# Copying the sum of an output norm out of PSUM before the inverse square root

## The chip, the cores and the metric

One core of one Trainium2 chip runs the kernel. The metric is device time in microseconds of one execution: 2615.6 us, the median of three runs (2614.31 to 2616.1). Engines are called as in the profile: PE is the matrix engine (PEld its weight load), DVE the vector engine, ACT the scalar engine, POOL the general-purpose engine, SP the one that issues most transfers.

## The reference

The block works on 1024 tokens of width 1024 in float32: a half-step SwiGLU, a mixer, a half-step SwiGLU, a final RMS norm. The mixer adds two gated branches. One is gated linear attention (GLA) with 4 heads of value width 256, the other a gated delta rule with 8 heads of width 128, both in chunks. The output of every head goes through an RMS norm before it is gated:

```
oh = o.reshape(b, t, heads, -1)
oh = oh * rsqrt(mean(oh * oh, axis=-1) + EPS) * w
```

Here is the place of the change: the mean over the channels of a head, and the inverse square root of it.

## The kernel before, in words

Activations are kept transposed, channels on the 128 partitions and tokens along the free dimension, so a sum over the channels of a head is a sum over partitions. `out_rms` (L801) forms it with a product by a matrix of ones: `sq` (128x512, the squares, which a DVE instruction at L1058 or L1184 has put together) goes in, and a PSUM bank `q` holds the sum on every partition. The scalar engine then takes the logarithm of `q` (L805), the exponential of minus half of it (L806) and the square of that (L807). The logarithm and the exponential each have a table load of their own ahead of them. Two DVE instructions make one Newton step: L808 reads `q` again, with the square, and L809 ends the factor `y`. The caller multiplies the head's output by it (L1060 or L1187).

`out_rms` is called 24 times. `delta_rec` (L1018) calls it twice for each of the 8 delta heads, once for each half of the tokens (some 870 to 1355 us of the trace). `gla_rec` (L1132) calls it twice for each of the 4 GLA heads (some 1424 to 1790 us).

**Banks of PSUM.** In the delta stage the pool has 4 banks of tag `q` and 2 tiles of two banks of tag `ps`. The `q` banks serve everything small: the steps of the recurrence (L1034, L1038, L1047), the output `qo` of half a head (held until L1060), the sum in `out_rms`, and, for the next head, the transposed keys (L897, read by ACT at L901 and by DVE at L903) and the scores of `delta_prep` (L923, read by DVE at L925 and L929). In the GLA stage there are 2 `q` banks, 4 banks of tag `m` for the large products (L368) and one `ps` tile. There, too, the scores (L1152), the transposed keys (L1146, read by ACT at L1147) and the steps of the state (L1170) share the `q` banks with `out_rms`. The helper `half()` gives SBUF tiles `h` of 128x512, 4 of them; `sq`, `t` and `y` are of that kind.

**What sets the order.** Each engine runs its instructions in a fixed order, which a planner lays down when the program is built: it goes by the order of the text, by its own estimate of every instruction's time, by priorities (`tc.high_priority`) and by when a buffer comes free. In some places the text pins an instruction behind another one (`pinned`, `tc.issue_after`): the scores at L923 go behind a set step of a dense projection (L139). So the dense products are laid between the small products of the recurrence, and a buffer that comes free at another time can change the order of everything behind it.

Of the kernel before, what the change touches and what calls it, by code (L numbers as in the profile page):

```python
# [10 lines left out]
AF = mybir.ActivationFunctionType  # L11
ALU = mybir.AluOpType
# [727 lines left out]
def mixer(st, sto, tc, pool, start, xs, load_unit, dense, ptile, bank, rsqrt_newton, split, new_x, accumulate,  # L740
          ounits, dram, pr, ident, ones, cst, eye, wlr, win, wout, y_d, h_d, sqrt_table, strassen_products, rp, psum, divide, recent, pinned, run):
    nc = tc.nc
# [36 lines left out]
    def half():  # L779
        return sp.tile([P, 512], F32, name="h", tag="h", bufs=4)  # L780
# [20 lines left out]
    def out_rms(sq):  # L801
        q = bank()
        nc.tensor.matmul(out=q, lhsT=ones, rhs=sq, start=True, stop=True)
        t, y = half(), half()
        nc.scalar.activation(out=t, in_=q, func=AF.Ln)  # L805
        nc.scalar.activation(out=y, in_=t, func=AF.Exp, scale=-0.5)  # L806
        nc.scalar.activation(out=t, in_=y, func=AF.Square)  # L807
        nc.vector.scalar_tensor_tensor(out=t, in0=q, scalar=-0.5, in1=t, op0=ALU.mult, op1=ALU.mult)  # L808
        nc.vector.scalar_tensor_tensor(out=y, in0=t, scalar=1.5, in1=y, op0=ALU.add, op1=ALU.mult)  # L809
        return y  # L810

# [208 lines left out]
    def delta_rec(kq, qsq, vt3, gl, kst, qk, cj, yi):  # L1020
# [4 lines left out]
        for b in range(2):  # L1025
            qo = bank()
            for n in range(4):
# [17 lines left out]
                if c < NCH - 1:  # L1045
# [5 lines left out]
                    else:  # L1051
# [5 lines left out]
            nc.scalar.activation(out=osq, in_=qo, func=AF.Square, scale=P ** -0.5)  # L1057
            nc.vector.scalar_tensor_tensor(out=osq, in0=osq, scalar=EPS * EPS, in1=qsq[:, cc], op0=ALU.add, op1=ALU.add)  # L1058
            fac = out_rms(osq)
            nc.vector.scalar_tensor_tensor(out=oT[:, cc], in0=qo, scalar=ph[:, 98:99], in1=fac,  # L1060
                                           op0=ALU.mult, op1=ALU.mult)
# [70 lines left out]
    def gla_rec(la, kt, f, vtok):  # L1132
# [5 lines left out]
        for b in range(2):  # L1138
# [41 lines left out]
            for a in range(2):  # L1180
                sq = half()
                nc.scalar.activation(out=sq, in_=qo[a], func=AF.Square, scale=1.0 / 16)
                sqs.append(sq)
            nc.vector.scalar_tensor_tensor(out=sqs[0], in0=sqs[0], scalar=EPS / P, in1=sqs[1], op0=ALU.add, op1=ALU.add)  # L1184
            fac = out_rms(sqs[0])
            for a in range(2):
                nc.vector.scalar_tensor_tensor(out=o[a][:, cc], in0=qo[a], scalar=ph[:, 96 + a:97 + a],  # L1187
# [57 lines left out]
    for b in range(2):  # L1245
        q = bank()
# [94 lines left out]
    for g in range(4):  # L1341
# [11 lines left out]
        for a in range(2):  # L1353
            t = 2 * g + a
# [120 lines left out]
```

## Time and profile before

| | |
|---|---|
| median of 3 runs | 2615.6 us (2614.31 to 2616.1) |
| the profiled execution | 2616.17 us, its span 2614.4 us |
| PE busy | 2491.3 us, 95% of the span |
| DVE busy | 1872.5 us, 72% |
| POOL busy | 1168.2 us, 45% |
| ACT busy | 1065.2 us, 41% |
| granted TensorE clock, mean | 0.986 |
| bytes moved | 75 GB/s over the span |

Read the shares as averages over stages. With PE at 95% what counts is where PE stands still and what ends each standstill; idle time of the other engines costs nothing unless PE waits for them. The tables of waits give, for an engine and a line, how long it stood before that line and what released it.

### The profile page before, as it was taken

The numbers are of one execution on the slowest core, as the hardware profiler recorded it, in microseconds if no ns is written. First come the engines' busy times: TensorE is split into PE (matmuls) and PEld (weight loads), VectorE is DVE, ScalarE is ACT, GpSimd is POOL, SyncE is SP. The second block draws the span as 40 slices with busy tenths as digits, with TensorE's granted clock in tenths as the row PEclk, the third lists the DMA queues.
The fourth block names the chain that finished last, engine by engine and source line by source line (L and its number), as shares of the span: only waits on it lengthen the run. The fifth ranks groups of instructions, "written<-read, shape, count | busy, mean of one in ns | idle before, by whom it ended". The sixth has DMA issues, their size and how long they took to land.

```text
span 2614.4 us, 32722 instructions
## 1 busy us (share of the span) xinstructions
PE 2491.3 (95%) x11668; PEld 2021.0 (77%) x11668; DVE 1872.5 (72%) x2900; ACT 1065.2 (41%) x1841; POOL 1168.2 (45%) x1308
## 2 busy tenths in 40 slices
PE   7899999899999999999989999999989999998998
PEld 6788888677877877777767777878868888886677
DVE  8855555899676778887596666757586555569996
ACT  5333334333353444444345544535233333343331
POOL 4544444555217567676452122122144444446531
PEclk8999999999999999999999999999989999999999
DMA  3222222322322222212211212124212222213222
GB/s 118 73 73 85 92 71 72 125 81 77 117 73 73 65 61 65 61 45 53 65 51 37 80 39 85 57 65 138 73 35 78 88 74 85 89 61 115 79 89 81
DMA packets 93603, 199.05 MB, mean 76 GB/s; under 512 B 12248, under 2 KB 17112, under 8 KB 93440
## 3 DMA queue, kind: packets, MB, share of 16 engines
q1 hardware_dynamic: 82576, 175.64, 20.7%
q0 software_dynamic: 8704, 18.89, 2.8%
q10 hardware_dynamic: 2160, 2.43, 0.3%
q8 instruction: 92, 1.51, 0.2%
q14 instruction: 71, 0.58, 0.1%
HBM read 158.73 MB, written 38.17 MB: 75 GB/s over the span
## 4 chain that ended last, share of the span: by engine, by line
PE 72%; DVE 14%; ACT 5%; issue 3%; POOL 1%; DMA 1%; DVEq 0%; POOLq 0%; ACTq 0%
PE q L368 28%; PE ps L139 17%; PE m L368 10%; PE q L575 7%; PE q L1001 2%; DVE wl L127 2%; PE q L923 1%; DVE h L580 1%; DVE xl L127 1%; DVE ha L580 1%; DMA s<-a_d 1%; ACT L806 1%; PE q L1014 1%; DVE acc L794 1%; PE ps L1163 1%
## 5 line engine op out<-in xcount | busy, mean ns | idle before, releaser
L127 DVE TENSOR_TENSOR wl<-raw,wh 128x512 fp32r<-128x512 f32 (+1 forms) x243 | 209.0, 860 | 169.7 <-ACT wh L126 168.0
L139 PE MATMUL ps<-xl,wh 128*128 128x512 f32 (+2 forms) x768 | 266.6, 407 | 18.6 <-ACT wh L120 8.2
L139 PE MATMUL ps<-xh,wl 128*128 128x512 f32 (+2 forms) x768 | 266.8, 406 | 0.1
L139 PE MATMUL ps<-xh,wh 128*128 128x512 f32 (+1 forms) x768 | 263.6, 405 | 0.0
L127 DVE TENSOR_TENSOR wl<-sr,wh 128x512 fp32r<-128x512 f32 x226 | 200.1, 886 | 73.4 <-ACT wh L126 72.9
L368 PE MATMUL q<-xl,wh 128*128 128x512 f32 x640 | 249.0, 389 | 0.3 <-ACT c L374 0.3
L368 PE MATMUL q<-xh,wh 128*128 128x512 f32 x640 | 249.0, 389 | 0.0
L368 PE MATMUL q<-xh,wl 128*128 128x512 f32 x640 | 249.0, 389 | 0.0
L126 ACT CAST wh<-sr 128x512 fp32r<-128x512 f32 x226 | 140.0, 620 | 242.2 <-PE q L575 63.5
L473 POOL TENSOR_TENSOR s<-s,ysc 128x512 f32<-128x512 f32 x80 | 112.4, 1416 | 244.1 <-ACT s L472 244.1
L126 ACT CAST wh<-raw 128x512 fp32r<-128x512 f32 (+1 forms) x243 | 144.1, 593 | 173.8 <-PE q L368 95.4
L139 PEld LDWEIGHTS ps<-xl,wh 128*128 128x128 f32 (+1 forms) x768 | 144.9, 193 | 51.2 <-DVE xl L239 8.9
L356 POOL TENSOR_TENSOR raw<-sr 128x512 f32<-128x512 f32 x19 | 25.6, 1347 | 318.1 <-DMA sr<-in_win 226.1
L139 PEld LDWEIGHTS ps<-xh,wl 128*128 128x128 f32 (+1 forms) x768 | 145.8, 193 | 25.6 <-issue 1.0
L139 PEld LDWEIGHTS ps<-xh,wh 128*128 128x128 f32 x768 | 144.4, 192 | 25.5 <-issue 1.2
L368 PEld LDWEIGHTS q<-xl,wh 128*128 128x128 f32 x640 | 120.1, 188 | 25.5 <-issue 0.7
L368 PEld LDWEIGHTS q<-xh,wl 128*128 128x128 f32 x640 | 120.1, 188 | 24.9
L368 PEld LDWEIGHTS q<-xh,wh 128*128 128x128 f32 x640 | 120.1, 188 | 24.9
L379 DVE TENSOR_TENSOR c<-c,q 128x512 f32<-128x512 f32 x120 | 82.4, 686 | 74.0 <-PE q L368 74.0
L374 ACT COPY c<-q 128x512 f32<-128x512 f32 x120 | 70.4, 587 | 152.6 <-PE q L368 150.7
L948 POOL TENSOR_TENSOR xp<-xp,itmp 128x112 f32<-128x112 f32 (+29 forms) x248 | 122.5, 494 | 19.4
L945 POOL TENSOR_TENSOR itmp<-lt,xp 128x112 f32<-128x112 f32 (+29 forms) x248 | 110.1, 444 | 38.7 <-DMA lt<-l_d 19.9
(494 smaller groups left out, 6775.6 us busy)
## 6 DMA issues: line engine op xcount, KB each, us to landing
sr<-in_win SPq DMA_DIRECT2D x76, 256.0 KB, 2.6
a_d<-s SPq DMA_DIRECT2D x36, 512.0 KB, 3.7
raw<-in_win SPq DMA_DIRECT2D x70, 256.0 KB, 2.6
raw<-in_d SPq DMA_DIRECT2D x56, 256.0 KB, 2.7
raw<-in_g SPq DMA_DIRECT2D x48, 256.0 KB, 2.6
s<-a_d SPq DMA_DIRECT2D x24, 512.0 KB, 4.1
sr<-in_u SPq DMA_DIRECT2D x44, 256.0 KB, 2.9
raw<-in_u SPq DMA_DIRECT2D x44, 256.0 KB, 2.6
```

What stands on the lines that cost most here:

```text
L126: a = nc.scalar.copy(out=hi, in_=src)
L127: b = (eng or nc.vector).tensor_sub(out=lo, in0=src, in1=hi.bitcast(F32))
L139: mm = nc.tensor.matmul(out=ps[:m, sl], lhsT=w[:, :m], rhs=x[:, sl], start=(i == 0 and a == 0), stop=(i == n - 1 and a == 2))
L368: nc.tensor.matmul(out=ps, lhsT=p[:, c], rhs=q, start=(first and k == 0 and a == 0), stop=(k == 3 and a == 2), skip_group_check=not first)
L374: marks[0] = nc.scalar.copy(out=t, in_=ps).ins
L379: marks[1] = nc.vector.tensor_add(out=t, in0=t, in1=ps).ins
L473: nc.gpsimd.tensor_mul(out=s, in0=s, in1=y)
L575: nc.tensor.matmul(out=ps, lhsT=p[:, c], rhs=q, start=(first and k == 0 and a == 0), stop=(k == 1 and a == 2), skip_group_check=not first)
L580: nc.vector.scalar_tensor_tensor(out=hd[:, sl], in0=ps, scalar=0.5, in1=hd[:, sl], op0=ALU.mult, op1=ALU.add)
L945: inv_eng.tensor_tensor(out=tv, in0=lp[:, j, j + 1:].unsqueeze(2).broadcast_to([P, r, m]), in1=xp[:, j, :m].unsqueeze(1).broadcast_to([P, ...
L948: inv_eng.tensor_tensor(out=xv, in0=xv, in1=tv, op=ALU.subtract)
L1001: nc.tensor.matmul(out=q[:, c], lhsT=lhs[:, c], rhs=rhs[:, c], start=True, stop=True)
```

## The change

Inside `out_rms` the sum is copied from the bank `q` into `sq`, whose content the product has then consumed, with one DVE instruction. The logarithm and the first Newton instruction read the copy in place of the bank. Nothing else differs.

```diff
     def out_rms(sq):
         q = bank()
         nc.tensor.matmul(out=q, lhsT=ones, rhs=sq, start=True, stop=True)
+        nc.vector.tensor_copy(out=sq, in_=q)
         t, y = half(), half()
-        nc.scalar.activation(out=t, in_=q, func=AF.Ln)
+        nc.scalar.activation(out=t, in_=sq, func=AF.Ln)
         nc.scalar.activation(out=y, in_=t, func=AF.Exp, scale=-0.5)
         nc.scalar.activation(out=t, in_=y, func=AF.Square)
-        nc.vector.scalar_tensor_tensor(out=t, in0=q, scalar=-0.5, in1=t, op0=ALU.mult, op1=ALU.mult)
+        nc.vector.scalar_tensor_tensor(out=t, in0=sq, scalar=-0.5, in1=t, op0=ALU.mult, op1=ALU.mult)
         nc.vector.scalar_tensor_tensor(out=y, in0=t, scalar=1.5, in1=y, op0=ALU.add, op1=ALU.mult)
         return y
```

## Rows read from the trace of the kernel before

**Rows 1.** The page's first part: busy time and share of the span by engine.
```profile
PE 2491.3 (95%) x11668; PEld 2021.0 (77%) x11668; DVE 1872.5 (72%) x2900; ACT 1065.2 (41%) x1841; POOL 1168.2 (45%) x1308
```

**Rows 2.** Busy time by window: stretch, its length, PE, PEld, DVE, ACT, POOL.
```profile
860.00:1370.00 510.00, 484.69 (x2626) 388.07 (x2624) 395.39 (x783) 224.56 (x406) 321.52 (x589) 0.99 0.21 59
1370.00:1810.00 440.00, 424.25 (x2002) 344.81 (x2001) 299.63 (x459) 216.32 (x348) 105.14 (x75) 0.99 0.21 67
```

**Rows 3.** PE's waits, 860 to 1370 us: releaser, total us, times, longest.
```profile
PE q L923 <- DVE h L808: 6.7, 6, 1.3
...
PE q L1038 <- DVE rw L1036: 3.7, 5, 1.0
```

**Rows 4.** PE's waits, 1370 to 1810 us.
```profile
PE q L1152 <- DVE h L808: 4.0, 3, 1.3
```

**Rows 5.** The chain that ended last, 860 to 1370 us, by line.
```profile
by line: PE ps L139 41.7%; PE q L1001 10.9%; PE q L923 4.4%; PE q L1038 2.9%; PE q L1014 2.8%; PE q L1042 2.6%; ACT L805 2.3%; ACT L806 2.3%; PE q L1034 2.1%; PE q L1047 2.1%; PE q L1044 2.0%; issue 1.7%; PE q L983 1.4%; DVE h L808 1.4%; DV
```

**Rows 6.** The timeline, second half of one delta head: start, length, engine, line.
```profile
955.69 1.02 PE L803 MATMUL q<-h,cs 128*128 128x512 f32 x2
...
956.82 2.02 DVE L988 TENSOR_TENSOR kq<-kq,gb 128x1792 f32<-128x1792 f32 x1
...
958.10 0.60 ACT L805 ACTIVATE h<-q 128x512 f32<-128x512 f32 x1
...
961.05 0.62 ACT L807 ACTIVATE h<-h 128x512 f32<-128x512 f32 x1
...
961.70 0.69 DVE L808 SCALAR_TENSOR_TENSOR h<-q,h 128x512 f32<-128x512 f32 x1 [2.86 <-ACT h L807]
...
962.36 0.69 DVE L903 TENSOR_TENSOR kst<-q,kdec 128x512 f32<-128x512 f32 x1
962.45 1.59 PEld L923 LDWEIGHTS q<-kq 128*128 128x128 f32 x8 [1.38 <-DVE h L808]
962.45 1.99 PE L923 MATMUL q<-kq 128*128 128x256 f32 x8 [0.96 <-DVE h L808]
```

**Rows 7.** The timeline, first half of a GLA head.
```profile
1644.10 1.12 PE L803 MATMUL q<-h,cs 128*128 128x512 f32 x2
...
1645.79 0.60 ACT L805 ACTIVATE h<-q 128x512 f32<-128x512 f32 x1
...
1648.22 1.57 DVE L127 TENSOR_TENSOR wl<-sr,wh 128x512 fp32r<-128x512 f32 x1 [2.42 <-ACT wh L126]
...
1650.83 0.69 DVE L808 SCALAR_TENSOR_TENSOR h<-q,h 128x512 f32<-128x512 f32 x1 [1.04 <-ACT h L807]
...
1651.57 1.16 PE L1152 MATMUL q<-la,lt 128*128 128x128 f32 x8 [1.34 <-DVE h L808]
```

**Rows 8.** The timeline, first half of a delta head.
```profile
1001.28 1.13 PE L803 MATMUL q<-h,cs 128*128 128x512 f32 x2
...
1002.04 0.74 DVE L794 SCALAR_TENSOR_TENSOR acc<-ps,ph,acc 128x511 f32<-128x511 f32 x1
...
1002.70 0.28 DVE L1036 TENSOR_TENSOR rw<-vt,q 128x128 f32<-128x128 f32 x1
...
1003.03 0.33 PEld L1038 LDWEIGHTS q<-rw,yi 128*128 128x128 f32 x2
```

**Rows 9.** Groups of DVE by line and shape: count, busy us, mean ns, idle before.
```profile
L809 DVE SCALAR_TENSOR_TENSOR h<-h 128x512 f32<-128x512 f32 x24 | 19.5, 812 | 0.4
...
L808 DVE SCALAR_TENSOR_TENSOR h<-q,h 128x512 f32<-128x512 f32 x24 | 16.5, 687 | 24.6 <-ACT h L807 24.6
...
L1173 DVE COPY Sg<-q 128x256 f32<-128x256 f32 x4 | 1.7, 424 | 0.1
...
L1217 DVE COPY yi<-ps 72x512 f32<-72x512 f32 x1 | 0.7, 680 | 0.0
```

**Rows 10.** Groups of ACT by line and shape.
```profile
L806 ACT ACTIVATE h<-h 128x512 f32<-128x512 f32 x24 | 15.2, 632 | 0.3
...
L805 ACT ACTIVATE h<-q 128x512 f32<-128x512 f32 x24 | 14.4, 598 | 1.5 <-PE q L803 1.3
```

## The prediction

> **What bounds the kernel now.** Read the busy shares first: PE is busy for 95% of the span and DVE for 72% [rows 1]. PE sets the time, so the change can give back only what PE now stands idle. The table by stretch says how much that is where `out_rms` runs: in the delta stage PE is busy 484.69 of 510 us, 25.3 us idle; in the GLA stage 424.25 of 440, 15.8 us idle [rows 2]. Next read PE's waits in these stretches. The largest single one of the delta stage is the scores at L923 waiting for DVE's L808: 6 times, 6.7 us [rows 3]; in the GLA stage the scores at L1152 wait for the same line, 3 times, 4.0 us [rows 4]. L808 makes nothing that the scores read. It is the last reader of the bank `q` of `out_rms`, so this is a wait for a free bank. The chain that ended last agrees: in the delta stage it goes through the two steps of the inverse root on ACT, L805 and L806 with 2.3% each, and L808 with 1.4% [rows 5].
>
> The timeline of one head shows why the bank is held. The sum is done at 955.69 + 1.02 = 956.71; the logarithm starts at 958.10, the square at 961.05, L808 at 961.70, and the scores at 962.45, PE having stood for 0.96 us [rows 6]. So the bank is kept for 962.39 - 956.71 = 5.7 us after the sum is there. In the GLA stage it is the same: sum done at 1645.22, L808 ends at 1651.52, PE idle for 1.34 us [rows 7].
>
> **The change part by part.** Durations are from the profiled execution of 2616.17 us (span 2614.4 us); it lies 0.6 us above the median of 2615.6, so I take 0.6 off the sum at the end.
>
> *The wait for the bank.* With the copy the bank comes free when the copy ends, some 0.7 us after the sum, in place of 5.7 us. That is before PE reaches the scores in all nine places. What can be won is bounded by 0 (another wait takes its place in full) and by the whole 6.7 + 4.0 = 10.7 us [rows 3, 4].
>
> For the GLA stage I take all 4.0: the scores' inputs are long there, and the product behind them (L1170) needs a key tile that ACT makes, not L808. For the delta stage I take 4.5 of 6.7, for this reason: L923 x8 is two groups of four, each with its own bank. The second group starts near 962.45 + 1.0 = 963.45, and its bank comes from L903, which ends at 962.36 + 0.69 = 963.05 [rows 6]. It has 0.4 us to spare. If PE comes 0.96 us earlier, it waits 0.96 - 0.4 = 0.56 us for L903 in the same place. If the planner keeps the two groups together, 6 x 0.56 = 3.4 us of the 6.7 come back, and 3.3 are won; if it parts them with dense products, as it can once a bank is free, all 6.7. I take 4.5, between the two.
>
> *The copy.* The trace has no copy of 128x512 out of PSUM on DVE. The nearest rows: 72x512 takes 680 ns, 128x256 takes 424 [rows 9]. By the row of the same length I take 0.68 us, 24 x 0.68 = 16.3 us more DVE work. What of it PE sees is unknown; the ends are 0 and 16.3. By place:
> - Second halves of the delta heads (8): DVE next runs L988 (2.02 us) and then stands still for 2.86 us before L808 [rows 6]. The copy fits in that gap. Cost 0 if it goes ahead of L988, since L988 ends before L808 can start either way.
> - First halves of the delta heads (8): here DVE feeds the recurrence. The sum ends at 1002.41; L1036 runs from 1002.70 to 1002.98, and PE loads its result at 1003.03 [rows 8]. A copy put ahead of L1036 starts after L794 (1002.78) and makes L1036 0.7 us late; put behind, it costs nothing there. PE already loses 3.7 us in 5 waits to L1036 [rows 3], so this path has no slack. Bounds 0 and 8 x 0.68 = 5.4; I take the half, 2.7, having no row that says which order the planner takes.
> - GLA halves (8): after the sum DVE stands idle, 2.42 us before L127 in the row shown [rows 7]. Cost 0, at most 8 x 0.68 = 5.4 if that gap is gone.
>
> *The logarithm waits for the copy.* It is queued on ACT ahead of the table load and exponential, and behind it stand the weight casts. In the GLA row it starts 0.57 us after the sum, in the delta row 1.39 us after [rows 6, 7]; a copy that starts with the sum's end costs it 0.1 to 0.2 us in the first and nothing in the second. Reading SBUF in place of PSUM makes it 632 - 598 = 34 ns longer, if it goes as the exponential [rows 10]: 24 x 0.034 = 0.8 us on an engine that is busy half of these stretches [rows 2]. I take 0 and keep 1 us.
>
> *L808 reads SBUF twice.* It then has the shape of L809, which takes 812 ns in the mean against 687 [rows 9]: 24 x 0.125 = 3.0 us of DVE. In the delta stage L808 is followed by L903, so some of it may show; I take 0 and keep 3.
>
> *The tile `sq`* is kept until L808 and not only until the product. Four `h` tiles exist, and `sq`, `t`, `y` make three, so one is left for the next user; I count nothing.
>
> Sum: - 4.0 - 4.5 + 2.7 = - 5.8 us, 2616.17 - 5.8 = 2610.4; less 0.6, **2609.8 us**.
>
> One rule speaks against the edit. The Trainium skill ("VectorE: DVE Perf Modes", Rules for kernel authors) says that elementwise work on a matmul's output should take PSUM as its source, or be copied out first if many operations follow. Here only two readers follow, and the rows show neither of them faster from SBUF (L809's mean is above L808's), so by that rule the copy is DVE work that buys nothing; it is the fourth rival below.
>
> **The rivals.**
> 1. *The whole wait goes.* The planner, given a free bank, spreads the scores between dense products and puts the copies where DVE idles. For it: DVE idles 24.6 us before L808 alone [rows 9]. Against it: the second bank above. - 10.7, and a first product that need not restart: 2616.2 - 10.7 - 0.6 = 2604.9.
> 2. *The wait moves.* PE stands for L903, or for the eviction behind L808, instead of for L808. The delta stage then wins nothing; GLA's 4.0 and the 2.7 of copies stay: - 1.3, 2614.3. For it: L903 ends only 0.66 us after L808 [rows 6].
> 3. *Slower: the copy queues behind L988.* In the second halves L988 starts 0.11 us after the sum. If it goes first, the copy ends at 958.84 + 0.68 = 959.5, and the logarithm starts 1.4 us later than now; so do L808 and, on DVE's fixed order behind it, L903. The second group of scores then waits 0.56 + 1.4 = 2.0 us in 6 heads, 11.8, against 6.7 won; with 4.0 won in GLA and the full 5.4 of the first halves: + 6.5, or 2622.1. It decides from some four of the six heads on. Against it: both are ready within 0.1 us, and the copy stands earlier in the text.
> 4. *The copy buys nothing.* All of DVE's 16.3 us lies on PE's path, because the planner's new order has less room between the small products; 10.7 are won: + 5.6, 2621.2. DVE is busy 78% of the delta stretch [rows 2], which speaks for part of it; its gaps around the copies speak against the whole.
>
> That the change does not do what it says is no real case: the bank has no other reader.
>
> **How the numbers follow.** No change means within 0.2%, 5.2 us, which is about what a measurement of this kernel can tell: 2610.4 to 2620.8. My forecast has 0.42, with a range of its own of 2607 to 2613, a little more than half of it under 2610.4; the first rival 0.15, the second 0.24, the third 0.12, the fourth 0.07. A new order of everything behind 870 us, which the planner may well lay down, adds some us of either sign to each; 2607 to 2613 is worked out from the bounds alone. Faster: 0.25 + 0.15 + 0.02 = 0.42. Slower: 0.09 + 0.05 + 0.02 = 0.16. The same: 0.42. The single figure stands just on the faster side. The range reaches from the first rival to the fourth: 2603.5 to 2621.
>
> **What would show it.** Right: no wait of L923 or L1152 for L808; L808's chain off the chain that ended last; 24 copies of 0.65 to 0.7 us, most in gaps; waits for L903 at L923 of some 2 us in total; PE idle in the two stretches down by about 6 us. Wrong: PE's waits for L903 or L925 as long as those now for L808 (rival 2); the copies behind L988 (rival 3); waits at L1038 and L1034 up by over 5 us, or PE idle up in the stretches though the wait is gone (rivals 3, 4); or a difference that sits outside 860 to 1810 us, which none of my steps explains.

## The result, and the profile after

The changed kernel takes 2629.3 us (median of 6 runs, 2627.75 to 2632.72) against 2616.3 in the runs of the kernel before beside them: ratio 1.0053, 95% interval 1.0043 to 1.0063, so 13 us slower. The forecast was 2609.8 us, and 2629.3 lies outside its range.

The line of busy shares answers to [rows 1]. PE is busy for 2.9 us more, DVE for 12.6:

```profile
PE 2494.2 (95%) x11668; PEld 2023.3 (77%) x11668; DVE 1885.1 (72%) x2924; ACT 1065.8 (41%) x1841; POOL 1173.6 (45%) x1308
```

The table by stretch answers to [rows 2], cut at the same instructions (columns: stretch, length, busy us of PE, PEld, DVE, ACT, POOL, then granted clock):

```profile
859.00:1382.80 523.80, 489.73 (x2625) 392.56 (x2624) 403.64 (x799) 224.90 (x406) 320.39 (x588) 0.98 0.21 58
1382.80:1822.60 439.80, 424.06 (x2002) 345.21 (x2001) 303.11 (x467) 216.46 (x348) 110.57 (x76) 0.99 0.21 67
```

The delta stage is 13.8 us longer, the GLA stage as long as before. Of the 13.8, PE idle is 8.8 (523.80 - 489.73 = 34.1, was 25.3), and 5.0 is PE busy longer with the same products. That second part is put down to the clock, below.

PE's waits in the delta stretch (releaser, us in total, times, longest), for [rows 3]; line numbers are one higher than before from L804 on:

```profile
PE q L924 <- DVE kst L904: 7.6, 6, 1.3
PE q L1043 <- DVE rw L1041: 5.0, 5, 1.8
PE q L1002 <- ACT h L1016: 4.4, 4, 2.4
PE q L1002 <- ACT h L1006: 4.2, 6, 0.7
...
PE q L1039 <- DVE rw L1037: 1.1, 2, 0.7
PE q L1015 <- DVE h L1008: 0.8, 3, 0.3
```

Two more rows of the kernel before stand against them:

```profile
PE q L1001 <- ACT h L1005: 2.9, 4, 0.7
...
PE q L1042 <- DVE rw L1040: 1.3, 2, 0.7
```

No wait for the root's last step is left, and the scores wait 7.6 us for the key tile in place of 6.7 for the root. The recurrence waits 5.0 us at L1043, up from 1.3, and 1.1 at L1039, down from 3.7. And the chain of small products at L1002 and L1015 waits for copies and subtractions: 4.4 us for ScalarE's L1016 and 0.8 for VectorE's L1008, rows that before did not have, and 4.2 for ScalarE's L1006, up from 2.9. So 6.5 of the 8.8 us of new idle time are waits in this chain; the scores have 0.9 of them and the recurrence 1.3. In the GLA stretch [rows 4] the 4.0 us have turned into two other waits:

```profile
PE ps L1164 <- DVE sc L1156: 3.1, 4, 0.9
PE q L1171 <- ACT kh L1148: 2.6, 4, 1.1
```

The chain that ended last in the delta stretch, by line, for [rows 5]. The root is still on it (L806, L807), and ScalarE's squares of the keys (L902) now stand beside it:

```profile
by line: PE ps L139 38.4%; PE q L1002 10.0%; issue 3.3%; PE q L1015 2.8%; PE q L1039 2.6%; PE q L1035 2.4%; PE q L1043 2.3%; ACT L807 2.0%; PE q L1048 1.9%; ACT jk L902 1.8%; PE q L1045 1.8%; PE q L803 1.7%; ACT L806 1.7%; PE q L924 1.7%; D
```

The second half of the delta head of [rows 6] (start, length, engine, line):

```profile
954.56 1.07 PE L803 MATMUL q<-h,cs 128*128 128x512 f32 x2
955.82 0.69 DVE L804 COPY h<-q 128x512 f32<-128x512 f32 x1
...
956.58 1.11 PE L924 MATMUL q<-kq 128*128 128x256 f32 x4
...
957.02 2.02 DVE L989 TENSOR_TENSOR kq<-kq,gb 128x1792 f32<-128x1792 f32 x1
957.97 0.63 ACT L806 ACTIVATE h<-h 128x512 f32<-128x512 f32 x1
...
962.27 0.69 DVE L904 TENSOR_TENSOR kst<-q,kdec 128x512 f32<-128x512 f32 x1
...
963.01 1.13 PE L924 MATMUL q<-kq 128*128 128x256 f32 x4 [1.22 <-DVE kst L904]
```

The copy ends 0.9 us after the sum, and the first group of scores begins 0.95 us after it in place of 5.74 [rows 6]. Then PE stands for 1.22 us at the second group, for L904. The GLA half that answers to [rows 7]:

```profile
1658.17 1.12 PE L803 MATMUL q<-h,cs 128*128 128x512 f32 x2
...
1659.33 0.69 DVE L804 COPY h<-q 128x512 f32<-128x512 f32 x1
...
1664.11 1.06 PE L1153 MATMUL q<-la,lt 128*128 128x128 f32 x8
```

The first half of a delta head, for [rows 8]. The copy goes ahead of the recurrence's subtraction:

```profile
1007.00 1.13 PE L803 MATMUL q<-h,cs 128*128 128x512 f32 x2
1008.30 0.68 DVE L804 COPY h<-q 128x512 f32<-128x512 f32 x1
...
1008.90 0.28 DVE L1037 TENSOR_TENSOR rw<-vt,q 128x128 f32<-128x128 f32 x1
```

The groups for [rows 9, 10]: 24 copies of 687 ns; the old L808, now L809, reads SBUF twice and takes 812 ns in the mean (a few long ones make this: the median is 692 ns, and was 688 from the bank); the logarithm L806 takes 632 ns and waits 8.7 us for copies in all.

```profile
L804 DVE COPY h<-q 128x512 f32<-128x512 f32 x24 | 16.5, 687 | 6.8 <-PE q L803 6.7
...
L809 DVE SCALAR_TENSOR_TENSOR h<-h 128x512 f32<-128x512 f32 x24 | 19.5, 812 | 16.0 <-ACT h L808 16.0
...
L806 ACT ACTIVATE h<-h 128x512 f32<-128x512 f32 x24 | 15.2, 632 | 8.9 <-DVE h L804 8.7
```

**Where the idle time came from.** Compare the chain of small products that ends the triangular inverse. Before, TensorE's timeline in one middle head:

```profile
1033.35 1.05 PE L1001 MATMUL q<-xb,n 128*128 128x128 f32 x8
1034.16 0.71 PE L139 MATMUL ps<-xh,wl 128*128 128x512 f32 x2
1034.71 0.63 PE L139 MATMUL ps<-xh,wh 128*128 128x512 f32 x2
1035.17 1.07 PE L1001 MATMUL q<-h,yb 128*128 128x128 f32 x8
1036.08 1.06 PE L1001 MATMUL q<-yb,h 128*128 128x128 f32 x8
1036.89 0.71 PE L139 MATMUL ps<-xl,wh 128*128 128x512 f32 x2
1037.53 1.08 PE L1014 MATMUL q<-h,n 64*64 64x128 f32 x8
```

And after, the same head:

```profile
1041.96 1.13 PE L1002 MATMUL q<-xb,n 128*128 128x128 f32 x8
1043.76 1.16 PE L1002 MATMUL q<-h,yb 128*128 128x128 f32 x8 [0.67 <-ACT h L1006]
1044.76 1.06 PE L1002 MATMUL q<-yb,h 128*128 128x128 f32 x8
1046.13 1.08 PE L1015 MATMUL q<-h,n 64*64 64x128 f32 x8 [0.32 <-DVE h L1008]
1047.89 1.16 PE L1002 MATMUL q<-h 64*128 64x128 f32 x8 [0.67 <-ACT h L1016]
```

Most products of the chain wait for a copy or a subtraction of the one ahead. Before, dense products (L139) fill these waits: from the transposes of the values (L983) to the last L1014 there are 11 to 12 of them in four middle heads. After, three of the middle heads have 0 or 1. The planner, whose order differs from the first norm on, has issued them earlier, and each such head shows gaps of 0.67, 0.25 or 0.32, and 0.67 us, 4.8 us in the three. The remaining middle head, at 970 us, is another case: it keeps 14 dense products, and one gap of 2.42 us for L1016 is new.

**Where the clock comes in.** In the head at 970 us PE stands for 2.42 us for L1016:

```profile
979.32 2.02 PE L1002 MATMUL q<-h 64*128 64x128 f32 x8 [2.42 <-ACT h L1016]
```

Then it runs 6.8 us at a granted clock of 0.50, the lower of its two levels (1.2 GHz), and after that at 1.00 (columns as in the table by stretch):

```profile
970.00:976.80 6.80, 6.80 (x49) 5.67 (x48) 5.79 (x12) 1.27 (x2) 2.56 (x5) 1.00 0.09 19
979.40:986.20 6.80, 6.80 (x27) 6.19 (x28) 5.53 (x10) 2.89 (x5) 3.73 (x10) 0.50 0.18 60
986.20:993.00 6.80, 6.80 (x45) 5.56 (x45) 5.11 (x9) 0.69 (x2) 6.01 (x11) 1.00 0.01 2
```

A second such stretch of 6.8 us lies at 1112, in one of the three bare chains (PE is busy for 6.1 us of it); before, the delta stage had one of 3.4 us at 1343, and both kernels have one at its end. At half the clock these make (6.8 + 6.1 - 3.4) / 2 = 4.7 us by estimate, near the 5.0. For the experiments I estimate the clock's part from the runs: the drop of the mean granted clock over a kernel's runs, times 2616 us (0.001 is 2.6 us; each run's clock is given to three places).

### The profile page after: what moved, and what is told of

The parts are those of the page before. It is cut to its first block, busy times and chain, and to the rows that moved or that the text cites. A ratio compares the mean times of both kernels' runs of the same rounds, so it can differ in the third digit from the quotient of the medians.

```text
span 2626.6 us, 32761 instructions
## 1 busy us (share of the span) xinstructions
PE 2494.2 (95%) x11668; PEld 2023.3 (77%) x11668; DVE 1885.1 (72%) x2924; ACT 1065.8 (41%) x1841; POOL 1173.6 (45%) x1308
## 4 chain that ended last, share of the span: by engine, by line
PE 69%; DVE 18%; ACT 6%; issue 4%; POOL 2%; DMA 1%; DVEq 0%; POOLq 0%; ACTq 0%; SPq 0%
PE q L368 28%; PE ps L139 17%; PE m L368 8%; PE q L575 6%; DVE wl L127 3%; PE q L1002 2%; DVE ha L580 1%; DVE xl L127 1%; DVE h L580 1%; DVE xl L239 1%; DMA s<-a_d 1%; ACT wh L126 1%; ACT L807 1%; DVE acc L794 1%; PE q L803 1%
## 5 line engine op out<-in xcount | busy, mean ns | idle before, releaser
L139 PE MATMUL ps<-xl,wh 128*128 128x512 f32 (+2 forms) x768 | 264.2, 407 | 18.0 <-ACT wh L120 8.0
L139 PE MATMUL ps<-xh,wl 128*128 128x512 f32 (+2 forms) x768 | 264.9, 405 | 0.1
L139 PE MATMUL ps<-xh,wh 128*128 128x512 f32 (+1 forms) x768 | 263.0, 403 | 0.0
L139 PEld LDWEIGHTS ps<-xl,wh 128*128 128x128 f32 (+1 forms) x768 | 143.4, 192 | 50.3 <-DVE xl L239 9.1
L139 PEld LDWEIGHTS ps<-xh,wl 128*128 128x128 f32 (+1 forms) x768 | 145.1, 192 | 26.2 <-issue 1.2
L139 PEld LDWEIGHTS ps<-xh,wh 128*128 128x128 f32 x768 | 144.4, 192 | 26.2 <-issue 0.9
L368 PEld LDWEIGHTS q<-xl,wh 128*128 128x128 f32 x640 | 120.1, 188 | 25.3 <-issue 0.4
```

What stands on the lines that cost most here:

```text
L139: mm = nc.tensor.matmul(out=ps[:m, sl], lhsT=w[:, :m], rhs=x[:, sl], start=(i == 0 and a == 0), stop=(i == n - 1 and a == 2))
L368: nc.tensor.matmul(out=ps, lhsT=p[:, c], rhs=q, start=(first and k == 0 and a == 0), stop=(k == 3 and a == 2), skip_group_check=not first)
```

## The experiments

Theory A: the edit itself costs little, and the loss is the order that the planner lays down with it. Theory B: the copies and the later logarithm hold up the work. "Order laid down" means that each engine's instructions are chained in that order, with no wait added. Differences are (ratio - 1) times 2616 us.

### Which stage: e4 and e5

```diff
-            fac = out_rms(osq)        # delta;  e4: edit in GLA alone
+            fac = out_rms(osq, False)
-            fac = out_rms(sqs[0])     # GLA;    e5: edit in delta alone
+            fac = out_rms(sqs[0], False)
```

> The edit in the GLA stage alone, planner free; the order of the delta stage is then that of the kernel before. The prediction's term for the GLA halves (the whole bank wait of 4.0 us comes back): 2612 us. Theory A, from the stretch in the trace of the changed kernel (440.0 before, 439.8 after; other waits took its place): 2615 to 2617 us. A loss of over 5 us here would go against both theories.

> The edit in the delta stage alone, planner free; the order of the delta stage is then that of the changed kernel. Both theories: 2626 to 2631 us, since the traces put the whole loss between 965 and 1240 us. If it stays under 2620 us, the loss is not of the delta stage, and both fall.

e4: 2618.8 us, ratio 1.0010 (1.0000 to 1.0020); that is 1.8 us above theory A's range, less than the interval's width, and the prediction's 2612 is out. e5: 2630.2, 1.0052 (1.0036 to 1.0067). The loss is the delta stage's. In GLA the bank wait is no gain at all: its 4.0 us reappear as waits for the scores' and the keys' copies.

### The order or the copies: e1, e2 and e7

```diff
 e1: every engine in the order of before, 16 copies in delta
 e7: the same, copies in the second halves alone
+            fac = out_rms(osq, b == 1)
 e2: every engine in the order of after, no copies; readers take sq
-        nc.vector.tensor_copy(out=sq, in_=q)
```

> The edit stands in the delta stage alone (16 copies), and every engine keeps the order of the kernel before, laid down instruction by instruction; each copy goes on VectorE in front of the first instruction that began, in the trace before, later than 0.3 us ahead of its sum's end. Theory A (the new order of the planner is the loss, the copies themselves are cheap): 2611 to 2618 us, the wait of the scores for the bank moves to L903/L904 and at most 3 us are won. Theory B (the 16 copies of 0.68 us and the logarithm that waits for them hold up the recurrence): 2624 to 2631 us, most of the 13 us are still lost, and PE's waits for the recurrence's subtraction and scaling are up by over 5 us.

> The order of the changed kernel on every engine, laid down instruction by instruction, with the copies left out; the logarithm and the last step of the root read the tile of squares itself, so the sum over channels doesn't enter the result. Theory A (order): 2624 to 2631 us, the loss stays without a single copy. Theory B (copies): 2610 to 2619 us.

> The order of the kernel before laid down on every engine, and copies only in the second halves of the delta heads (8, all ahead of L988 or its like), where the bank wait of the scores is. Theory A1 (at the old order the loss of 6 us comes from the copies of the first halves, which stand in front of the recurrence): 2613 to 2618 us. Rival (the copies ahead of L988 or the logarithm that waits for them cost it): 2620 to 2625 us.

e2, without a copy: 2630.0 us, 1.0051 (1.0036 to 1.0067), the whole loss; 6.4 us of it is clock by the estimate (0.9840 against 0.9864). Its waits are those of the changed kernel:

```profile
PE q L923 <- DVE kst L903: 8.3, 6, 1.5
...
PE q L1001 <- ACT h L1015: 4.4, 4, 2.4
```

e1: 2622.6 us, 1.0024 (1.0014 to 1.0034), between the theories: 6 us of direct cost that A had not foreseen. e7: 2618.8, 1.0010 (1.0001 to 1.0018), 0.8 us above A1's range and under the rival's. So at the old order the copies of the first halves account for the difference, 0.0014 or some 4 us (the intervals overlap, so the size is rough), and those of the second halves win nothing: in e7 the scores still wait 3.9 us for L903 and 2.3 for the output at L1060, 6.2 in place of 6.7. A and B are both partly right, but the parts don't add: within the new order the copies cost nothing that shows (e5 and e2 have 1.0052 and 1.0051, each to about 0.0015). e2 frees the bank early too, as the change does, so it shows the order to be the cause, and not yet what in the edit makes the order.

### What the chain's cover is worth: e6, e9 and e13

```diff
 e6: kernel before, TensorE, six heads
-L983 x8 | 1 L139 | L1001 | 4 L139 | L1001 L1001 | 2 L139 | L1014 | 4 L139 | L1001 ...
+11 L139 | L983 x8 | L1001 | L1001 L1001 | L1014 | L1001 ...
 e9: order of after, ScalarE, at 977 us
-L120 | L798 | L791 | L1016
+L1016 | L120 | L798 | L791
 e13: the whole change, TensorE alone in the order of before
```

> The kernel before, without the edit and with its own order on every engine, save one thing on TensorE: in six heads the 11 to 21 dense products that stand between the transposes of the values and the last small product of the inverse are issued ahead of these transposes, as the planner does it in the changed kernel. Theory A (the changed kernel loses because the chain of small products at L1001 has no dense products left to cover the copies that it waits for): each head loses the three gaps that the changed kernel shows there, 0.67 + 0.32 + 0.67 = 1.66 us, six heads 10 us: 2622 to 2629 us. Rival (a dense product issued earlier is never lost, PE gets the gap back later): 2614 to 2619 us.

> The order of the changed kernel laid down on every engine, save one thing on ScalarE: in one head (978 us in its trace) the copy of the small product's result (L1016) goes ahead of a cast, a tanh and a scaling (L120, L798, L791) that stood before it. Theory A (in that place PE stood for 2.42 us and then ran for 6.8 us at the lower clock): 1.7 us of gap and some 3 us of lower clock come back, 2622 to 2626 us. Rival (the chain is bound elsewhere, the gap moves to the next wait): 2627 to 2632 us.

> The whole change with its 24 copies, TensorE held to the order of the kernel before, the other engines as the planner puts them. Theory A (what the changed kernel loses is TensorE's new order; copies cost some 4 us in the first halves): 2616 to 2623 us. Rival (the new orders of VectorE and ScalarE lose it): 2625 to 2635 us.

e6: 2629.4 us, 1.0054 (1.0042 to 1.0066). A kernel without the edit, with nothing moved but dense products to an earlier place, loses as much as the change (0.4 us above A's range). It bares the chain in six heads and the change in three, so e6 shows that a bare chain can cost this much, and that the two losses are equal is in part chance. The row L1001 <- L1015 is new and L1001 <- L1005 is up from 2.9:

```profile
PE q L1001 <- ACT h L1005: 8.4, 12, 0.7
PE q L923 <- DVE h L808: 6.4, 6, 1.3
PE q L1001 <- ACT h L1015: 4.0, 6, 0.7
```

5.5 + 4.0 = 9.5 us agrees with the delta stretch, which is 10.6 us longer in the profile, with 9.6 us more idle. The timed runs have a mean clock of 0.9848 against 0.9872, which is 6 of the 14 us by the estimate and leaves 8 for the gaps.

e9 went to the rival: 2631.2, 1.0068 (1.0054 to 1.0081). The 2.42 us gap went, and in the same place PE now waits 2.6 us with a dense product, for the scaling that was moved back (L791) and VectorE's instruction behind it:

```profile
PE ps L139 <- DVE acc L794: 2.6, 1, 2.6
```

e13 went against theory A too: 2635.6, 1.0072 (1.0055 to 1.0089), with the old cover and 0.6 us above the rival's range. So TensorE's order alone is not the answer. The planner then fits VectorE and ScalarE in otherwise: the scores wait 8.7 us for L903, and the product at L1042 waits 5.4 us for the scaling (1.3 before). Its profiled execution, at a clock of 0.987, shows only 9 us of the loss (span 2623.3); over its runs the clock goes down to 0.982.

### Why the freed bank buys nothing: e8, e10, e11 and e12

```diff
 e8: e7, VectorE, six heads
-copy | L988 | L808 | L903 | L809 | ... | L903
+copy | L988 | L903 | L903 | L808 | L809
 e10: kernel before, TensorE, six heads
-16 L139 | L923 x8 | 3 L139 | L923 x8 | 15 L139 | L983
+20 L139 | L923 x8 | 3 L139 | L923 x8 | 11 L139 | L983
 e11: e10, and 3 more L139 from ahead of L983 into the 0.73 us gap at L1001
 e12: e7, and 4 L139 from ahead of L983 between the first two groups of L923
```

> As the copies of the second halves alone at the old order, and in six heads both multiplications of the key tiles (L903) go on VectorE ahead of L808, into the gap in which it stood idle for 2.4 us. Theory (the wait that took the place of L808 is L903, queued on VectorE behind L808 and L809): the second bank comes free earlier and PE's wait at the scores falls from some 6 us to under 3: 2609 to 2614 us. Rival (the second bank is held by ScalarE's squares, which read it too, and not by L903): the wait stays, 2613 to 2618 us.

> The kernel before without the edit, its own order on every engine, save that in the six heads in which PE waits for the bank of L808, four dense products (L139) that stood behind the scores are issued ahead of them. Theory A (the wait for the bank costs only what no dense product covers): PE does 4 x 0.227 = 0.9 us of its work in each wait, 6.7 us of waits fall to under 2, and nothing else moves: 2609 to 2613 us. Rival (the products taken from behind the scores covered VectorE's step to the transposes, the wait moves there): 2614 to 2618 us.

> As the one with four dense products ahead of the scores, and in the four heads in which the chain at L1001 still shows a gap of 0.73 us, three more dense products from the same stretch go into that gap. Theory A: a further 4 x 0.7 = 2.8 us come back: 2606 to 2611 us. Rival (the stretch ahead of the transposes has no products left to give, they now wait for L929): no better than with the four alone, or worse.

> Copies in the second halves of the delta heads alone, at the old order, and in six heads four dense products from behind the scores are issued between the first group of scores (whose bank the copy frees) and the second (whose bank L903 and ScalarE's squares hold). Theory A (the copy only moves the wait by one group; with cover it is gone either way): 2610 to 2615 us, no better than the same cover without copies. Rival (the earlier bank is worth something by itself): under 2609 us.

e8: 2625.7 us, 1.0039 (1.0027 to 1.0051), worse than either theory: at the scores PE waits 5.3 us for L903, as long again for L905 and 1.5 for L1060, 12.1 in all. VectorE's timeline shows L903 standing for the squares of the keys on ScalarE (L901), and L808 now queued behind it, at 1028.59:

```profile
1026.38 0.69 DVE L903 TENSOR_TENSOR kst<-q,kdec 128x512 f32<-128x512 f32 x1 [3.02 <-ACT jk L901]
1027.98 0.69 DVE L903 TENSOR_TENSOR kst<-q,kdec 128x512 f32<-128x512 f32 x1 [0.91 <-ACT jk L901]
1028.59 0.68 DVE L808 SCALAR_TENSOR_TENSOR h<-h 128x512 f32<-128x512 f32 x1
```

These squares stand in ScalarE's queue among the logarithm, the exponential, the square and two table loads of 1.28 us. That queue sets when the second bank comes free, and the copy shortens nothing on it. In e8 moving L903 ahead won no time and delayed L808 and what stands behind it.

e10: 2616.9, 1.0000 (0.9992 to 1.0009), the rival. The wait at the scores falls from 6.7 to 1.3 us as meant, and 4.5 us turn up one step on:

```profile
PE q L983 <- DVE em L929: 4.5, 6, 0.9
...
PE q L923 <- DVE h L808: 1.3, 4, 0.4
```

e11: 2619.6, 1.0010 (1.0002 to 1.0019), the same wait at 7.2 us. e12: 2615.6, 0.9993 (0.9984 to 1.0001), with 4.5 us as e10 has; by the ratio it is in A's range, by the median 0.6 us above. So the bank wait was one link of a chain that goes through ScalarE's queue, the scores, L929 and the transposes; filling or freeing one link hands its wait to the next. The lowest times are e12's, and they are not shown to be below those of the kernel before. e10 and e12 also give no sign that laying an order down costs time by itself.

### What in the edit takes the cover away: e14 to e17

```diff
 e14: planner free, delta only
+            fac = out_rms(osq, b == 1)
 e15:
+            fac = out_rms(osq, b == 0)
 e16: kernel before, and after the product
+        nc.vector.memset(sq, 0.0)
 e17: the change, but the root's last step keeps the bank
-        ...scalar_tensor_tensor(out=t, in0=sq, scalar=-0.5, ...
+        ...scalar_tensor_tensor(out=t, in0=q, scalar=-0.5, ...
```

> The change in the second halves of the delta heads alone (8 copies), planner free. In the plan that it lays down, the chain of small products from the values' transposes to L1014 keeps 10 dense products in each of the four middle heads (11 to 12 in the kernel before, 0 to 1 in three of them in the changed one). Theory A (the loss comes when the dense products leave that chain, and the copies of the first halves make them leave): 2612 to 2620 us, no loss. Rival (any copy in the delta stage gives the planner an order that loses): 2624 to 2632 us.

> The change in the first halves of the delta heads alone (8 copies), where no bank wait was, planner free; the chain keeps 4 dense products in three of the middle heads, 8 in the other. Theory A (the copy in front of the recurrence costs some 4 us by itself, and the plan some more by the bare chain): 2622 to 2630 us. Rival (the loss belongs to the second halves, where the bank comes free earlier): 2613 to 2619 us.

> The kernel before with a fill of the tile of squares (128x512, on VectorE, read by nobody) in the place of each of the 24 copies; logarithm and last step read the bank as before, which is held as before. Planner free; the chain keeps 4 to 5 dense products in the middle heads. Theory A (VectorE's time in the first halves makes the planner spend the dense products on the recurrence; the freed bank has no part in it): 2621 to 2630 us. Rival (the early bank, and with it the early scores, is what changes the order): 2613 to 2619 us.

> All 24 copies, the logarithm reads them, but the last step of the root (L808) still reads the sum in the bank, so the bank is held as long as before. Planner free; the chain keeps 2 dense products in the middle heads. Theory A: 2624 to 2632 us, as the change itself, with the bank wait of L808 still there. Rival (the freed bank drives the loss): 2613 to 2620 us.

| | copies in delta | bank freed early | L139 in the chain, middle heads | ratio (95%) | clock's part |
|---|---|---|---|---|---|
| e14 | second halves | yes | 10, 10, 11, 11 | 0.9998 (0.9987 to 1.0010) | 1 us |
| e15 | first halves | yes | 8, 4, 4, 4 | 1.0032 (1.0019 to 1.0045) | 8 us |
| e16 | 24 fills | no | 5, 4, 4, 4 | 1.0044 (1.0028 to 1.0060) | 12 us |
| e17 | all | no | 2, 2, 2, 2 | 1.0026 (1.0013 to 1.0038) | 1 us |

e14, e15 and e17 lie in theory A's ranges, e16 0.9 us above. But the kernel before took 2618.4 us beside these runs; by the ratio e17 comes to 2622.8 us, short of A's 2624, so it bears A out only in part. Where the bank wait was, copies are harmless with the planner free, and the scores wait 7.3 us for L903 as in the changed kernel (e14). An instruction more on VectorE in the first halves (e15 has it there alone), where no bank wait was, makes the planner spend the dense products on the recurrence: from the chain's end to the last sum of a middle head there are 107 to 111 of them in e15 to e17, 98 to 101 in the kernel before and 96 to 100 in e14. A fill of 485 ns that nobody reads loses 11.5 us. It also keeps the tile `sq` a little longer, as the copies do; no run parts this from VectorE's time. e16's loss is nearly all clock by the estimate, and e15's too. Behind gaps of 0.89 and 0.67 us in one chain with few dense products left, e16's profile has:

```profile
966.00:976.50 10.50, 8.94 (x59) 7.41 (x58) 8.94 (x31) 2.92 (x6) 2.78 (x5) 1.00 0.20 61
976.50:993.60 17.10, 16.37 (x60) 13.75 (x60) 10.12 (x16) 3.46 (x6) 13.18 (x27) 0.50 0.11 32
```

e17 loses half of what the change does (6.8 us, against 13.9 by the ratio). That the other half comes of the freed bank is possible and not shown, since the two orders differ everywhere.

## Why the prediction was wrong

- **The step that failed** is "a new order of everything behind 870 us ... adds some us of either sign to each". It stood outside the sum, and it was the result: 13 us without a single copy (e2). I had counted what DVE and PE do around each sum, and not what covers the next small products. Of the 13.8 us in the delta stretch 8.8 is idle and 5.0 goes to the clock. 6.5 of the 8.8 are waits in the chain of small products, 2.4 of them the one gap for L1016. e6 shows that baring this chain costs time by itself (9.5 us of waits in six heads), and e15 and e16 beside e14 show in which halves the added instruction brings it about. "PE idle up in the stretches though the wait is gone" was named as what would show it wrong, and did.
- **The wait for the bank, - 4.5 in delta.** Measured: + 0.9 in the changed kernel (7.6 for 6.7), - 0.5 at the old order (e7). The prediction saw the second bank and gave it 0.56 us per head, from L903's end. What it missed is that L903 follows ScalarE's queue, so this bank comes no earlier when PE does: in the half at 962 us L904 stands right behind L809, which waited 2.24 us for L808's square, and in three other places it waits for the keys' squares themselves (5.1 us; 3.02 and 0.91 in e8). Rival 2 was right on this point. The Trainium skill ("PSUM — Partial Sum Buffer", PSUM bank collisions raise a hardware error) says that two engines may not touch one bank in the same partitions at the same time, reads included, so the two readers of a bank have to take turns; e8's rows agree, with 3.02 us for which VectorE stood.
- **The bank wait, - 4.0 in GLA.** Measured: 0 in the stretch, + 2.6 us (0 to 5.2) in e4. The product behind the scores does wait for the key tile from ScalarE: 2.6 us at L1171, which I had called no obstacle.
- **The copies, + 2.7.** Right in place and kind: first halves, ahead of L1036, 0.68 us each. At the old order they cost some 4 us (e1 less e7), inside the bounds of 0 to 5.4 as far as the overlapping intervals tell. Second halves and GLA halves were put at 0; for the former e14 agrees (0.9998), and e7 leaves 2.6 us (0.3 to 4.7).
- **The logarithm and L808.** From SBUF the logarithm takes 632 ns, as forecast. It stands 8.7 us for the copies in all, more than the 0.1 to 0.2 us a place that I had named for GLA; e2 has no copies to wait for and the same loss, so this wait is not its cause. L808 takes 3.0 us more in all, as forecast, but not by its shape: the median stayed (692 ns for 688).
- **The copy behind L988 (rival 3)** does not occur in the half shown: the copy at 955.82 goes ahead at 957.02.
- **All 16.3 us on PE's path (rival 4).** That this time lies on PE's path is refuted by e2, though the figure, 2621.2, lay on the right side. Its reason, a new order with less room between the small products, came nearest to what the runs show. On the rule of the Trainium skill ("VectorE: DVE Perf Modes", Rules for kernel authors) beside it, to copy out of PSUM first if many operations follow, the rows agree that the copy buys nothing for two readers: the medians of 692 ns from SBUF and 688 from the bank are alike, and no kernel with the copy is shown to be faster than the one before.
- **The clock** was in no term. Two stretches of 6.8 us at 1.2 GHz behind PE's new gaps took some 5 us. The Trainium skill ("TensorE: Matmul & The Clock Gate", A second HAM failure mode: psum-queue depth-cycling) tells of short standstills between groups of matmuls that make the clock swing between its levels; e16's rows agree (17.1 us at 0.50 behind gaps of 0.89 and 0.67 us), e6's do not (1.00 behind gaps of 0.68 and 0.67).
- **The range's lower end,** 2603.5, is 1.4 us under the first rival's 2604.9, and no term of the prediction gives the difference.

Open: how much of the new order's loss the recurrence and VectorE's order bring (e13 has the old cover and loses more), what part the freed bank has, and how the 13 us divide between the three bare chains, the one gap of 2.42 us and the clock from run to run.

## What to carry to other kernels

A bank wait is worth what the chain behind it gives back: before pricing it, ask what holds the next bank and the next operand, and move some dense work into the wait to see whether it only goes one link on. Where a planner lays down the order, the dense products that cover a chain of small ones are the thing to count before and after; a cheap instruction on the engine that feeds another chain can draw them off, and a run with the new order and without the edit parts the two. Even in the second halves alone, where the bank wait was, the copy won nothing (e14 0.9998, e7 1.0010).

## What was not expected of the hardware

Gaps well under a microsecond, a few in one chain, stand ahead of the lower clock level in e16, as one gap of 2.42 us does in the changed kernel; e6's profile has such gaps (0.68, 0.67 and 0.73 us between 974 and 983) and a granted clock of 1.00 from 970 to 990, and two of the changed kernel's three bare chains have no such stretch, so they do not always bring it. With the clock the runs of one kernel spread: e13 took 2625.15 us at a granted clock of 0.987 and 2641.29 at 0.982, 16 us apart, of which 0.005 x 2616 = 13 us is the clock by the estimate. The profile shows the clock of one execution alone, and so a loss of this kind can be missing from it.
